# Routing on VectorE alone in four batches, the expert lists made later, and the buffers of the last loads changed, in a two-layer mixture-of-experts trunk

## The chip, the cores and the metric

The kernel runs on one core of one Trainium2 chip. The metric is the device time of one execution in microseconds (us). A core has TensorE (matmuls and transposes; the profile calls it PE, and PEld its weight loads), VectorE (DVE), ScalarE (ACT), GpSimd (POOL) and SyncE (SP). SP issues the plain DMA transfers here, GpSimd the indirect ones (gathers and scatters by a list of indices). Each engine runs its own queue in order.

## The reference

A decoder trunk of two layers over 1024 tokens of width 1024, in float32. Layer 0 mixes the tokens with a gated DeltaNet beside an S5 state space model, layer 1 with dilated attention. After each mixer comes `x = LayerNorm(alpha * x + mixer(x))`, and then the part in question, a mixture of experts in two levels:

```
group_prob = softmax(xt @ wg_r + bg_r);  p_group, group = top_k(group_prob, 1)
in_group   = the 8 logits of (xt @ we_r + be_r) that belong to the group
top_logit, top_local = top_k(in_group, 2)
gate   = p_group * softmax(top_logit);  expert = group * 8 + top_local
y      = sum over the two experts of gate * (silu(x @ w_gate[e]) * (x @ w_up[e])) @ w_down[e]
x      = LayerNorm(alpha * x + y)
```

There are 32 experts with an inner width of 512, so each has 6 MB of float32 weights, and 2048 pairs of token and expert per layer, 64 for an expert in the mean.

## The kernel before, in words

Both layers go through the same stages. **The mixer** fills most of the time that the experts don't take; the change leaves it alone.

**The output stage** (`out_stage`, L816) takes 8 tiles of 128 tokens. For each it adds the residual (L851), takes the row statistics, transposes the tile on TensorE, computes the 36 router logits (`logits`, L250; the sum that ends it is L259), normalizes the tile (`layer_norm`, L217) and stores it to `hd` in main memory. The norm's first step is on ScalarE, its second on VectorE and its third on GpSimd; for the last tile ScalarE takes the second step's scale, and GpSimd both the product with the norm's gain (L223) and the sum (L226). `route` (L261) works on a batch of tiles: for each token the best group and the two best experts by chains of compare and reduce on VectorE (`top`, L279 to 291), the token's rank within its expert by matmuls with a triangle of ones, and the place of its number in a table, with one-hot matrices (L333, L335). `BATCH = {3: 0, 6: 4, 7: 7}` says after which tile a batch is routed and where it begins: tiles 0 to 3, 4 to 6, and 7. The last batch writes the token lists of the first FIXED experts (L353 to 355) and marks the instruction `R["end"]`.

Then come, all in this stage: `sort` (L359), which ranks the 32 experts by count with VectorE ops and matmuls of TensorE and writes the order of the experts and the lists of all others; `gates` (L395), the gate of each pair and its place in a table in memory, with two products on GpSimd (L417); and `overflow` (L682), a chain of small VectorE ops and two matmuls (L712) that lists the blocks of tokens that don't fit.

**The experts** (`moe`, L606). Experts 0 and 1 (FIXED = 2) go first, in fixed order, so that they need no order. The 14 next largest are large like them, up to 128 tokens a pass: each weight tile of 1 MB is split into a high and a low half of fp32r, by a copy on ScalarE (L486) and a difference on VectorE (L489), and each product is three matmuls (L528, L529, L546). The first weight tile's differences go to GpSimd (L488). The 16 others are small: 64 tokens, float32, no split (L583, L599), gathered two at a time in one list. The order is: the fixed ones, then in turn two small and two large. Each expert's rows are gathered from `hd` by an indirect DMA on GpSimd (L495), transposed (L503), and its result is scattered to `yd` by another (L551, L602). After the scatter of the fourth expert, GpSimd issues the 16 scatters of the table (`table`, L422).

All 192 weight tiles of a layer are loaded by SP at L458, in the experts' order, into 17 buffers in turn: RAW = 10 on the left of SBUF, then RAWB = 7 on the right (L455). At most two, later three loads are in flight. For experts past the fixed ones SP first reads the expert's number from the order (L625), and waits for it.

**The join.** A loop over overflow blocks (`moe_rest`, L660) makes no pass with this input, but its start holds all engines at a barrier (L668). Ahead of it stand the loads of the value weights of the attention (`value_loads`, L911, four tiles of 1 MB into buffers of the right ring, layer 0), the loads of rows of `h` (`ahead`, L717) and the splits of the value weights (`value_weights`, L920, through the common `split`, L446: copy L449, difference L450). `combine` (L730) then loads for each token tile its two experts' rows (L738) and normalizes their sum. In layer 0 VectorE adds them (L774, L775), and transposes (L794) and value matmuls follow; in layer 1 TensorE adds them with diagonal matrices (L758), for the odd tiles with alpha times `h` in the same sum (SUMMED). The norm squares the row on ScalarE (L778) and scales it in place on VectorE (L779), then finishes it (L782).

The framework places the instructions: it orders each engine's queue ahead of time by a simulated timeline, sets the semaphores from the tiles' data, and a buffer is free when its last reader is done. `issue_after(x)` keeps instructions behind `x` in that order.

Of the kernel before, what the change touches and what calls it, by code (L numbers as in the profile page):

```python
# [13 lines left out]
I32 = mybir.dt.int32  # L14
# [18 lines left out]
FIXED = 2  # L33
# [5 lines left out]
BATCH = {3: 0, 6: 4, 7: 7}  # L39
# [114 lines left out]
class Trunk:  # L154

    SUMMED = (1, 3, 5, 7)

# [59 lines left out]
    def layer_norm(self, r, mv, g, b, adder, spare=False):  # L217
# [141 lines left out]
    def sort(self, R, first, small, order, ps):  # L359
# [3 lines left out]
        w = R["sort"]  # L363
        key, hot, tmp, tab = w[:NE, 0:32], w[:NE, 32:64], w[:NE, 64:96], w[:NE, 128:256]
        kp, rank = w[:NE, 96:97], w[:NE, 97:98]
        ident = self.ident[:NE, :NE]
        nc.vector.scalar_tensor_tensor(key, R["cnt"][:NE], float(NE), self.c("keyb")[:NE], op0=OP.mult, op1=OP.add)
# [6 lines left out]
        nc.tensor.transpose(p[:NE, :128], R["tab"], self.ident)  # L374
# [8 lines left out]
        nc.vector.tensor_copy(R["rank"], p[:, 96:128])  # L383
# [11 lines left out]
    def gates(self, R, lg, gate, place, wk):  # L395
# [71 lines left out]
    def weights(self, src):  # L467
# [11 lines left out]
        for c in range(2):  # L479
# [126 lines left out]
    def moe(self, l, hd, yd, first, small, order, place, xp, wk, ps):  # L606
# [32 lines left out]
        next(run)  # L639
        next(run)  # L640
        for i in range(NE):
# [12 lines left out]
            if i == 3:  # L654
                with tc.issue_after(st.ins):
                    self.table(l, place)

# [24 lines left out]
    def overflow(self, R, over, ps):  # L682
# [3 lines left out]
        w = R["sort"][:BLOCKS]  # L686
        cap, c, cum, one, le, f = (w[:, i * NE:(i + 1) * NE] for i in range(6))
        ci = R["over"][:BLOCKS]

        idx = self.c("pidx")[:BLOCKS]  # L690
        nc.vector.tensor_scalar(cap, R["rank"][:BLOCKS], float(LARGE) - 0.5, None, op0=OP.is_lt)
# [1403 lines left out]
```

## Time and profile before

| | |
|---|---|
| three runs | 2487.99, 2479.51, 2486.32 us |
| median of the runs | 2486.32 us |
| the profiled execution's own time | 2481.84 us |
| its span in the trace | 2480.0 us |
| mean granted clock of TensorE | 0.961 of full speed |
| busy: TensorE, its weight loads | 2247.2 us (91%), 1629.5 us (66%) |
| busy: VectorE, ScalarE, GpSimd | 1468.4 (59%), 1143.1 (46%), 488.4 us (20%) |
| transfers | 560.83 MB, mean 226 GB/s |

Busy shares are means over the whole span. In it the stretches alternate: in the experts' two stretches, some 545 us each, the transfers run at about 405 GB/s, and in the mixers mostly at 30 to 270. So a share says little of what binds in one stretch, and the rows below are read from stretches: windows of time, the timeline of one engine, and the chain of waits. In a timeline row, the bracket at the end is the engine's idle time ahead of the instruction and what released it; `x8` at the end of the operation says that eight like ones in a row are told as one.

### The profile page before, as it was taken

The page shows a single profiled execution, that of the slowest core. Times are in us where ns is not written, and L with a number is a line of the kernel's source. Part 1 is how long each engine was busy: PE and PEld are TensorE (multiplying, and loading weights), DVE is VectorE, ACT ScalarE, POOL GpSimd, SP SyncE. Part 2 cuts the span into 40 slices and gives each one's busy share as a digit, 9 for nine tenths or more (in the row PEclk, how much of TensorE's full clock was granted, in tenths as well). Part 3 has the DMA queues.
Part 4 walks back from the last instruction along what each step waited for, and adds up shares of the span by engine and source line. Part 5 has one row for each costly group of instructions (what it writes and reads, how often), then busy time and mean ns, then how long its engine had stood idle before and what let it go on. Part 6 is the DMA issues. An engine that isn't in the chain of part 4 may idle for free. (4 is left out here: it accounts for less than half of the span.)

```text
span 2480.0 us, 34001 instructions
## 1 busy us (share of the span) xinstructions
PE 2247.2 (91%) x11950; PEld 1629.5 (66%) x11950; DVE 1468.4 (59%) x2901; ACT 1143.1 (46%) x1871; POOL 488.4 (20%) x566
## 2 busy tenths in 40 slices
PE   7999999889697999999599999998987799999995
PEld 5888899678454555555377888886865555555552
DVE  7655656556853555555553777777567544555545
ACT  5435453442543444444323666667224444444442
POOL 1445434102222111110001111113121311111000
PEclk9999999999698999999799999999988999999998
DMA  4222222272499999999631000102817999999976
GB/s 164 61 65 43 64 82 59 101 267 111 178 390 383 411 406 405 398 405 405 215 123 44 33 30 32 41 25 85 319 59 289 370 415 405 408 408 405 404 286 254
DMA packets 179199, 560.83 MB, mean 226 GB/s; under 512 B 59200, under 2 KB 96448, under 8 KB 129360
## 3 DMA queue, kind: packets, MB, share of 16 engines
q1 hardware_dynamic: 163920, 525.01, 55.6%
q0 software_dynamic: 15104, 33.60, 3.5%
q8 instruction: 96, 1.57, 0.3%
q14 instruction: 79, 0.65, 0.1%
HBM read 518.76 MB, written 55.36 MB: 231 GB/s over the span
## 5 line engine op out<-in xcount | busy, mean ns | idle before, releaser
L489 DVE TENSOR_TENSOR wlo<-wraw,whi 128x1024 fp32r<-128x1024 f32 x380 | 447.9, 1220 | 142.5 <-ACT whi L486 139.2
L486 ACT ACTIVATE whi<-wraw 128x1024 fp32r<-128x1024 f32 x384 | 384.3, 1054 | 74.6 <-PE pu L529 34.6
L583 PE MATMUL pgs<-wraw,xs 128*64 128x512 f32 x1024 | 241.8, 604 | 0.0
L583 PEld LDWEIGHTS pgs<-wraw,xs 128*64 128x64 f32 x1024 | 69.6, 138 | 133.1 <-issue 126.7
L172 PE MATMUL pj<-xTh,phi 128*128 128x512 f32 x320 | 131.0, 414 | 13.3 <-ACT xTh L449 13.3
L1073 POOL TENSOR_TENSOR plo<-praw,phi 128x256 fp32r<-128x256 f32 x64 | 53.0, 829 | 411.0 <-ACT phi L1072 282.1
L172 PE MATMUL pj<-xTh,plo 128*128 128x512 f32 x320 | 132.2, 414 | 0.0
L172 PE MATMUL pj<-xTl,phi 128*128 128x512 f32 x320 | 130.5, 408 | 0.0
L528 PE MATMUL pg<-whi,xh 128*128 128x512 f32 x256 | 107.4, 419 | 20.3 <-ACT whi L486 15.2
L599 PE MATMUL pos<-wraw,hs 128*64 128x512 f32 x512 | 118.6, 598 | 5.1 <-ACT xh L449 3.3
L172 PE MATMUL opo<-ohi,oyp 128*128 128x512 f32 x392 | 115.5, 403 | 2.4 <-DVE oyp L450 2.4
L1089 PE MATMUL pj<-xTh,phi 128*128 128x512 f32 x256 | 114.8, 448 | 2.2 <-DVE KL L1105 1.0
L528 PE MATMUL pg<-wlo,xh 128*128 128x512 f32 x256 | 108.4, 423 | 8.5 <-DVE wlo L489 8.3
L975 ACT ACTIVATE sm<-sm,st 128x1024 f32<-128x1024 f32 (+7 forms) x128 | 99.2, 775 | 36.4 <-DVE st L974 34.9
L551 POOL DMA_INDIRECT yd<-ot,first x32 | 38.8, 1214 | 368.3 <-issue 155.9
L971 DVE CUSTOM_DVE_ANT_0 sm<-s,amask 128x1024 f32<-128x1024 f32 (+7 forms) x128 | 96.4, 755 | 20.9 <-PE s L967 19.0
L988 PE MATMUL pp<-cf,sm 128*128 128x128 f32 x576 | 94.0, 274 | 11.7 <-ACT yt L1013 4.3
L528 PE MATMUL pg<-whi,xl 128*128 128x512 f32 x256 | 103.9, 406 | 0.0
L529 PE MATMUL pu<-wlo,xh 128*128 128x512 f32 x256 | 102.9, 402 | 0.0
L529 PE MATMUL pu<-whi,xl 128*128 128x512 f32 x256 | 102.7, 401 | 0.0
L529 PE MATMUL pu<-whi,xh 128*128 128x512 f32 x256 | 102.4, 400 | 0.0
L1089 PE MATMUL pj<-xTh,plo 128*128 128x512 f32 x256 | 101.5, 397 | 0.1
(543 smaller groups left out, 5148.1 us busy)
## 6 DMA issues: line engine op xcount, KB each, us to landing
wraw<-in_wm SPq DMA_DIRECT2D x384, 1024.0 KB
cy<-yd SPq DMA_DIRECT2D x32, 512.0 KB
praw<-in_win SPq DMA_DIRECT2D x40, 256.0 KB
oraw<-in_wo SPq DMA_DIRECT2D x16, 512.0 KB
hd<-or SPq DMA_DIRECT2D x16, 512.0 KB
ca<-hd SPq DMA_DIRECT2D x16, 512.0 KB
praw<-in_wqk SPq DMA_DIRECT2D x64, 128.0 KB
oy<-ytd SPq DMA_DIRECT2D x14, 448.0 KB
```

What stands on the lines that cost most here:

```text
L172: self.last = self.nc.tensor.matmul(*args, **kw).ins
L486: nc.scalar.activation(hi, r[:, h], AF.Copy)
L489: eng.tensor_tensor(lo, r[:, h], hi.bitcast(F32), op=OP.subtract)
L528: nc.tensor.matmul(pg, x[:, k], w[:, 0:512], start=s, stop=z)
L529: nc.tensor.matmul(pu, x[:, k], w[:, 512:1024], start=s, stop=z)
L583: nc.tensor.matmul(pg[r].rearrange("p (g f) -> p g f", g=2), x[:, k], w[:, k % 2, a], start=(k == 0), stop=(k == KT - 1))
L599: nc.tensor.matmul(po[r], hs[:, f % 2, f // 2], W[f // 2][:, o:o + 512], start=(f == 0), stop=(f == 3))
L971: nc.vector.tensor_tensor_reduce(out=sm[:, :n], in0=s[:, :n], in1=am[:, 1024 - n:1024], scale=1.0, scalar=-3e38, op0=OP.add, op1=OP.max, a ...
L975: nc.scalar.activation(sm[:, :n], sm[:, :n], AF.Exp, bias=st[:, 1:2], accum_out=st[:, 2:3])
L988: nc.tensor.transpose(pp[:, (j - j0) * 128:(j - j0 + 1) * 128], sm[:, j * 128:(j + 1) * 128], self.ident)
L1073: nc.gpsimd.tensor_tensor(lo, r, hi.bitcast(F32), op=OP.subtract)
L1089: nc.tensor.matmul(p, w[:, o], x[:, k, cs], start=(k == 0 and i == 0), stop=(k == KT - 1 and i == 2))
```

## The change

What it does, part by part:

- **Routing.** Four batches in place of three (tiles 0 to 3, 4 and 5, 6, and 7). In `out_stage` a tile's norm and its store now stand ahead of its batch's routing. The last tile's norm is made like the others', with its sum on VectorE. The gates' product and the first weight tile's differences go from GpSimd to VectorE.
- **Late lists.** `sort` is issued in `moe` behind the first expert's gather and its split, and `overflow` behind the table, after the fourth expert; what they read is kept in a tile `ov` that outlives the output stage. FIXED goes from 2 to 3, so the fourth expert, behind which the table is issued, is the first small one.
- **Ring.** The last five weight tiles (from 187 on) use the right ring's buffers. The value weights are loaded straight into `V`, on the left, and split ahead of the loop. The rows of `h` stand first in their pool on the left.
- **Join.** The norm writes its scaled row into `y[:, 1]`, which held the second expert's row, and no longer in place. In layer 1 the loads of the norm's gain and bias, the diagonal matrices, and alpha times `h` for tiles 0 to 3 on TensorE stand ahead of the tiles, and SUMMED is gone.

The diff, cut to its core:

```diff
-FIXED = 2
+FIXED = 3
...
-BATCH = {3: 0, 6: 4, 7: 7}
+BATCH = {3: 0, 5: 4, 6: 6, 7: 7}
...
         last = nc.scalar.activation(r, r, AF.Identity, bias=mv[:, 8:9])
-        if spare:
-            last = nc.scalar.activation(r, r, AF.Copy, scale=mv[:, 7:8])
-            nc.gpsimd.tensor_tensor(r, r, g, op=OP.mult)
-        else:
-            nc.vector.scalar_tensor_tensor(r, r, mv[:, 7:8], g, op0=OP.mult, op1=OP.mult)
+        nc.vector.scalar_tensor_tensor(r, r, mv[:, 7:8], g, op0=OP.mult, op1=OP.mult)
         return last, adder.tensor_tensor(r, r, b, op=OP.add)
...
-            nc.gpsimd.tensor_tensor(M, M, self.c("eidx")[:, None, :].to_broadcast([128, NT, NE]), op=OP.mult)
+            nc.vector.tensor_tensor(M, M, self.c("eidx")[:, None, :].to_broadcast([128, NT, NE]), op=OP.mult)
...
-        raw = self.raw_ring[self.at % len(self.raw_ring)]
+        n = len(self.raw_ring)
+
+        raw = self.raw_ring[self.at % n if self.at < NE * 6 // n * n else -1]
...
-            eng = nc.gpsimd if self.at == 1 else nc.vector
-            with after(eng):
-                eng.tensor_tensor(lo, r[:, h], hi.bitcast(F32), op=OP.subtract)
+            with after(nc.vector):
+                nc.vector.tensor_tensor(lo, r[:, h], hi.bitcast(F32), op=OP.subtract)
...
+        with tc.issue_after(self.hold["x"].ins):
+            self.sort(ov, first, small, order, wk, ps)
         next(run)
...
             if i == 3:
                 with tc.issue_after(st.ins):
                     self.table(l, place)
+                    self.overflow(ov, over, wk, ps)
...
+        P = {}
+        if l:
+            self.bcast_rows(g, self.I["lnfg"][l], D)
+            self.bcast_rows(b, self.I["lnfb"][l], D)
+            al = wk.tile([128, 128], F32, name="al", bufs=1)
+            nc.vector.tensor_scalar(al, self.ident, ALPHA, None, op0=OP.mult)
+            dg = wk.tile([128, NT, 2, 128], F32, name="cdg", bufs=1)
...
+            for u in range(4):
+                P[u] = ps.tile([128, D], F32, name="cp", tag="cp", bufs=4)
+                for c in range(2):
+                    h = slice(c * 512, (c + 1) * 512)
+                    nc.tensor.matmul(P[u][:, h], al, rows[u][:, h], start=True, stop=False)
...
-                if t in self.SUMMED:
-                    terms = [(al, a)] + terms
...
-                if t in self.SUMMED:
+                if t in P:
                     nc.scalar.activation(a, p, AF.Copy, accum_out=st[:, 0:1])
...
-            nc.vector.scalar_tensor_tensor(a, a, st[:, 1:2], g, op0=OP.add, op1=OP.mult)
+            nc.vector.scalar_tensor_tensor(y[:, 1], a, st[:, 1:2], g, op0=OP.add, op1=OP.mult)
...
-            nc.vector.scalar_tensor_tensor(a, a, st[:, 8:9], b, op0=OP.mult, op1=OP.add)
+            nc.vector.scalar_tensor_tensor(a, y[:, 1], st[:, 8:9], b, op0=OP.mult, op1=OP.add)
...
+            act, _ = self.layer_norm(r, mv, g, b, nc.vector if t == NT - 1 else nc.gpsimd)
+            nc.sync.dma_start(hd[ts, :], r)
             if t in BATCH:
                 self.route(BATCH[t], t + 1, R, lg, first, wk, ps)
-            act, add = self.layer_norm(r, mv, g, b, nc.gpsimd, t == NT - 1)
-            nc.sync.dma_start(hd[ts, :], r)
-        R["sort"] = wk.tile([128, KT * 128], F32, name="osort", tag="orT", bufs=1)
         with self.tc.issue_after(R["end"].ins):
-            self.sort(R, first, small, order, ps)
             self.gates(R, lg, gate, place, rp)
-            self.overflow(R, over, ps)
-        self.hold = {nc.scalar: act, nc.gpsimd: add, nc.vector: R["end"]}
+        self.hold = {nc.scalar: act, nc.vector: R["end"]}
...
-    def value_loads(self):
-        R = []
+    def value_weights(self, V, vp):
+
+        W = []
         for a in range(4):
-            r = self.raw_ring[0].tile([128, 2048], F32, name="wraw", tag="wraw")
+            r = V[:, 2 * a:2 * a + 2]
             with self.tc.issue_after(self.flight[-1]):
-                self.nc.sync.dma_start(r, self.I["wv"][a])
...
+                self.nc.sync.dma_start(r.rearrange("p c n -> p (c n)"), self.I["wv"][a])
...
-                        R = self.value_loads()
+                        W = self.value_weights(V, vp)
                     else:
                         vp = alloc("cr")
-
-                        vp.tile([128, 8192 + (NE * 6 % (RAW + RAWB)) * 2048], F32, name="used")
-                    there = self.ahead(l, hd, vp, range(NT if l else 2))
+                    rows = [vp.tile([128, D], F32, name=f"ca{t}") for t in range(NT if l else 2)]
+                    g, b = (vp.tile([128, D], F32, name=n) for n in ("fg", "fb"))
+                    self.ahead(l, hd, rows)
                     self.moe_rest(l, hd, yd, over, xg, wk, ps)
-                    if l == 0:
-                        W = self.value_weights(R, vp)
```

## Rows read from the trace of the kernel before

**Rows 1.** Window in the experts: us, PE, PEld, DVE, ACT, POOL, PEclk, DMA share, GB/s

```profile
700.00:720.00 20.00, 18.36 (x85) 10.72 (x82) 8.40 (x12) 7.51 (x10) 2.27 (x2) 1.00 1.00 403
```

**Rows 2.** Waits in the experts, layer 0: us, times, longest

```profile
SPq L458 <- DMA wraw<-in_wm: 382.1, 169, 4.1
...
PEld pgs L583 <- DMA wraw<-in_wm: 4.7, 15, 0.4
```

**Rows 3.** VectorE's timeline, end of layer 0's routing: start us, us, instruction

```profile
618.54 0.26 DVE L259 SCALAR_TENSOR_TENSOR lg<-lgd,ln_mv,orb 128x36 f32<-128x36 f32 x1
...
625.90 1.63 DVE L259 SCALAR_TENSOR_TENSOR lg<-lgd,ln_mv,orb 128x36 f32<-128x36 f32 x1
...
627.73 2.29 DVE L300 SCALAR_TENSOR_TENSOR rt<-rM,rt 128x96 f32<-128x96 f32 x1
...
629.94 4.71 DVE L317 TENSOR_TENSOR rt<-rM,cf 128x96 bf16<-128x96 f32 x2
...
642.84 0.17 DVE L355 TENSOR_SCALAR first<-first 128x2 int32<-128x2 int32 x1
...
643.19 1.21 DVE L489 TENSOR_TENSOR wlo<-wraw,whi 128x1024 fp32r<-128x1024 f32 x1
...
649.75 0.16 DVE L691 TENSOR_SCALAR osort<-rrank 24x32 f32<-24x32 f32 x1
...
653.08 0.14 DVE L709 TENSOR_SCALAR osort<-osort 24x1 f32<-24x1 f32 x1
```

**Rows 4.** GpSimd's timeline, the same stretch, and layer 1's first gather

```profile
625.11 2.36 POOL L223 TENSOR_TENSOR or<-or,og 128x1024 f32<-128x1024 f32 x1 [5.58 <-ACT or L222]
627.55 2.35 POOL L226 TENSOR_TENSOR or<-or,ob 128x1024 f32<-128x1024 f32 x1
629.87 4.68 POOL L489 TENSOR_TENSOR wlo<-wraw,whi 128x1024 fp32r<-128x1024 f32 x2
...
643.29 3.44 POOL L495 DMA_INDIRECT xg<-hd,first  x1 [1.06 <-DVE ge L408]
...
1866.51 3.34 POOL L495 DMA_INDIRECT xg<-hd,first  x1 [1.04 <-DVE ge L408]
```

**Rows 5.** TensorE's timeline, the first expert's transposes

```profile
653.44 1.97 PE L503 MATMUL px<-cf,xg 128*128 128x128 f32 x8
```

**Rows 6.** SP's timeline, and transfers in 640 to 660 by half microseconds

```profile
650.26 37.61 SPq L458 DMA_DIRECT2D wraw<-in_wm  x14
...
GB/s 0 0 0 0 0 0 0 0 0 0 0 0 0 0 58 74 139 156 49 0 0 0 164 33 229 410 459 410 426 442 393 426 459 410 410 393 377 442 270 271
```

**Rows 7.** GpSimd's and TensorE's timelines around the table, layer 0

```profile
721.58 1.26 POOL L602 DMA_INDIRECT yd<-ots,small  x1 [3.73 <-ACT ots L601]
...
733.80 1.59 POOL L428 DMA_INDIRECT tab<-tokv,place  x1 [0.30 <-issue]
...
756.28 1.05 POOL L495 DMA_INDIRECT xg<-hd,small  x1 [0.30 <-DMA tab<-tokv,place]
...
765.59 1.94 PE L503 MATMUL px<-cf,xg 128*128 128x128 f32 x8 [13.98 <-DMA xg<-hd,small]
```

**Rows 8.** Timelines of ScalarE, SP, VectorE and TensorE at layer 0's join

```profile
1197.44 7.67 ACT L449 ACTIVATE vhi<-wraw 128x1024 fp32r<-128x1024 f32 x8
...
1208.05 0.80 SPq L738 DMA_DIRECT2D cy<-yd  x2
...
1216.24 1.28 DVE L779 SCALAR_TENSOR_TENSOR ca<-ca,fst,fg 128x1024 f32<-128x1024 f32 x1 [1.31 <-ACT cy L778]
...
1222.97 1.97 PE L794 MATMUL ct<-cf,ca 128*128 128x128 f32 x8 [26.12 <-DMA cy<-yd]
```

**Rows 9.** The chain that ended last, and a window of layer 1's join

```profile
2419.40 8.50 DMA fb<-in_lnfb
...
2432.42 36.67 PE cp L758 x80
...
2450.00:2460.00 10.00, 10.00 (x25) 4.46 (x24) 9.37 (x22) 5.13 (x10) 0.00 (x0) 1.00 0.55 222
```

More of the change, by code (lines that the diff above doesn't have):

```diff
@@ L154 @@
 class Trunk:
-    SUMMED = (1, 3, 5, 7)
     def __init__(self, tc, I, out):
@@ L604, in small, with moe @@
             in_=ot, in_offset=None, bounds_check=4 * S - 1, oob_is_err=False)
-    def moe(self, l, hd, yd, first, small, order, place, xp, wk, ps):
+    def moe(self, l, hd, yd, first, small, order, place, ov, over, xp, wk, ps):
         nc, tc = self.nc, self.tc
@@ L680, in moe_rest, with overflow @@
                 pass
[L682 removed]
+    def overflow(self, ov, over, wk, ps):
         nc = self.nc
[L686 to L688 removed]
+        w = wk.tile([NE, 256], F32, name="ovw", tag="ovw", bufs=1)[:BLOCKS]
+        cap, c, cum, one, le, f, ci = (w[:, i * NE:(i + 1) * NE] for i in range(7))
+        ci = ci.bitcast(I32)
+        cnt, rank = ov[:BLOCKS, 0], ov[:BLOCKS, 1]
         idx = self.c("pidx")[:BLOCKS]
[L691 to L692 removed]
+        nc.vector.tensor_scalar(cap, rank, float(LARGE) - 0.5, None, op0=OP.is_lt)
+        nc.vector.scalar_tensor_tensor(c, cap, -64.0, cnt, op0=OP.mult, op1=OP.add)
         nc.vector.tensor_scalar(c, c, 63.0, 0.0, op0=OP.add, op1=OP.max)
@@ L715, in overflow, with ahead @@
         nc.vector.tensor_copy(over[:, 2, 0:1], cum[0:1, NE - 1:NE])
-    def ahead(self, l, hd, p, ts):
+    def ahead(self, l, hd, rows):
         nc = self.nc
-        g, b = (p.tile([128, D], F32, name=n) for n in ("fg", "fb"))
-        rows = {}
         with self.tc.issue_after(self.flight[-1]):
-            for t in ts:
-                rows[t] = p.tile([128, D], F32, name=f"ca{t}")
-                nc.sync.dma_start(rows[t], hd[t * 128:(t + 1) * 128, :])
+            for t, r in enumerate(rows):
+                nc.sync.dma_start(r, hd[t * 128:(t + 1) * 128, :])
                 if l == 0:
-                    nc.scalar.activation(rows[t], rows[t], AF.Copy, scale=ALPHA)
-        return g, b, rows
+                    nc.scalar.activation(r, r, AF.Copy, scale=ALPHA)
     def combine(self, l, hd, yd, gate, g, b, rows, wk, ps, done):
@@ L763, in combine @@
             else:
-                if t in rows:
+                if t < len(rows):
                     a = rows[t]
@@ L814, in out_products, with out_stage @@
                     yield MM, 0
-    def out_stage(self, l, ytd, W, last, po, first_ps, xd, hd, gate, first, small, order, place, over, rp, wk, wp,
+    def out_stage(self, l, ytd, W, last, po, first_ps, xd, hd, gate, first, place, ov, rp, wk, wp,
                   part):
@@ L1983, in run @@
                 with self.pool(f"ow{l}", 2) as wk, self.pool(f"owp{l}") as wp:
-                    self.out_stage(l, ytd, *out, xd, hd, gate, first, small, order, place, over, pools[2], wk, wp,
+                    self.out_stage(l, ytd, *out, xd, hd, gate, first, place, ov, pools[2], wk, wp,
                                    pools[0])
@@ L1993, in run @@
                     self.part_ring = [pools[0]] * 4 + [partb] * 2
-                    xg = self.moe(l, hd, yd, first, small, order, place, xp, wk, ps)
+                    xg = self.moe(l, hd, yd, first, small, order, place, ov, over, xp, wk, ps)
                     for q in reversed(pools):
@@ L2025, in run @@
                     nc.scalar.activation(wk.tile([128, 1], F32, name="warm", bufs=1), self.ident[:, 0:1], AF.Sqrt)
-                    self.combine(l, hd, yd, gate, *there, wk, ps, done)
+                    self.combine(l, hd, yd, gate, g, b, rows, wk, ps, done)
                 vp.release()
```

47 lines of the change are left out of this document (16 added, 31 removed).

## The prediction

> **What bounds the kernel now.** I read the page first and found four stretches in each layer: the mixer, an output stage that ends in routing, the experts, and the join of their rows. The edits sit where one stretch ends and the next starts, so the question for each is which wait ends last there.
>
> In the experts' stage TensorE is busy 18.36 of 20 us and the DMA engines all the time, at 403 GB/s [rows 1]. SP's loads wait for earlier loads, 382.1 us in the first layer, so they are paced by the transfers and not by free buffers; yet the weight loads of TensorE waited only 4.7 us for those transfers in 545 us [rows 2]. Both run at nearly one speed with a cushion of loaded tiles between them. So what starts TensorE earlier, or takes a hole out of its work, moves the end of the stage, as long as the transfers move too.
>
> Ahead of that stage the routing is held up on VectorE. The sum of the logits that took 0.26 us a tile earlier takes 1.63 us, the next op 2.29 and the next two 4.71 [rows 3]. They end at 627.53, 630.02 and 634.65, and GpSimd's ops end at 627.47, 629.90 and 634.55 [rows 4]: each VectorE op waited out a GpSimd op on the same memory. The first expert's list is ready at 643.01 [rows 3], the gather starts at 643.29 [rows 4], its data move from 647 to 649.5 (the slices of half a microsecond in the GB/s row) [rows 6]. But the first transposes start at 653.44 with no wait for a transfer shown [rows 5]: ahead of them in TensorE's queue stood the matmuls of the sort and of the overflow list, whose chain of 17 VectorE ops ran from 649.75 to 653.22 [rows 3]. SP loaded nothing more until 650.26 [rows 6], because it stood at the load of the sorted order. Layer 1 repeats all this 1223.2 us later; its first gather takes 3.34 us [rows 4].
>
> Later, 16 scatters of the table (733.80 to 756) stand on GpSimd's queue ahead of a gather, and TensorE waits 13.98 us for it [rows 7].
>
> At the join of layer 0 the splits of the value weights run on ScalarE from 1197.44 for 7.67 us; only then come the loads of the experts' rows (1208.05), and TensorE stands still for 26.12 us [rows 8]. At the end of layer 1 the loads of the rows wait for the bias row (8.50 us), then TensorE works 36.67 us [rows 9].
>
> **The change, part by part.** All sums are against the profiled execution, 2481.84 us: a span of 2480.0 and 1.84 around it. The median of the three runs, 2486.32, lies 4.48 above it.
>
> *Routing and first gather.* The last tile's norm goes to VectorE: a scale (1.28 us) and a sum (about 1.2, as a weight difference of that size took 1.21 [rows 3]), ready when ScalarE has made one pass over the tile, some 1.2 us ahead of GpSimd's start at 625.11 [rows 4]. So the logits come at 626.8 in place of 625.9 plus 1.63. GpSimd's 2.36 + 2.35 + 4.68 us [rows 4] leave the stretch. What is left of the routing took 8.4 us from 634.6 to 643.0; with tiles 4 and 5 in a batch of their own, and no lock, it is some 15 dependent ops at 0.20 us (17 ops in 3.47 us [rows 3]) and 2 us for ranks and table: 5.2 at least, 8.4 at most, I take 6.4. The list is ready at 633.2, 9.8 earlier. The gather lands 6.2 us after its start at best (643.29 to 649.5) and 10.15 at most (653.44) [rows 4 to 6]; nearest to the data's end I take 7.2, and TensorE starts at 640.7, 12.7 earlier. With the ends: 7.8 to 14.9. I book **12.5 per layer, 25**. The extra batch is some 26 short ops beside TensorE's matmuls, where VectorE is half idle: nothing; without that cover 5 us per layer.
>
> *Late lists.* The sort moves behind the first gather's split, the overflow list behind the fourth expert, and SP's load of the order behind the loads of experts 0 to 2 (the third fixed expert needs no list). SP's queue then holds seven free buffers' worth of loads from about 627. On VectorE the two lists stand between weight differences, on TensorE between matmuls; a weight part is made up to six halves ahead, 8 us of matmuls, which hides their 7 us of VectorE time. At nothing hidden, 23 dependent ops each behind one difference of 1.2 us cost 28 us per layer; at full cover 0. I take the cover: **-1.5 per layer, -3**.
>
> *The table.* It is issued after the fourth expert. With three fixed ones that is the first small expert of a pair, not the second: its scatter came at 721.58 where the table started at 733.80 [rows 7], 12 us earlier as seen from the next gather. The scatter of the second small one now falls behind the table (1.3 us), so the gather comes 9 us earlier as against TensorE, and of the 13.98 us some 5 stay. Below: none is won, if the order on the queue swaps; above: 14. I take **9 per layer, 18**.
>
> *Loads at the end, layer 0.* The last five weight tiles use the seven right buffers, so they wait for the experts before them (until about 1181 on today's clock), and the value weights come behind them, later than now; but their splits no longer wait for the left buffers to be free of TensorE's last matmuls. The last of four tiles lands near 1197, its split ends near 1201, and the barrier at 1202 in place of 1207.8: 5.7. The scale beside the squares, into another tile, takes the 1.31 us wait out of the first tile's chain [rows 8]. Holding the row buffer longer delays the third tile's load by 5 us, behind 11 us of matmuls per tile: nothing; without that cover 5 us once. **7**, from 0 to 8.
>
> *Loads at the end, layer 1.* The eight rows and the two norm rows no longer wait for the buffers of the last weights and start, by the loads ahead of them on SP, some 6 us earlier; so the expert rows start at about 2422 in place of 2427.9, when the bias row is there (2419.40 + 8.50 [rows 9]). Sixteen of TensorE's 80 matmul records go ahead of them into that wait, but then VectorE binds: it is busy 9.37 of 10 us [rows 9] and keeps its work, four tiles at 3.4 us and four at 4.6, 32 us. **6**, from 3 to 10.
>
> Sum: 25 - 3 + 18 + 7 + 6 = 53, and 2481.84 - 53 = **2428.8 us**.
>
> **A rule that speaks against it.** The first gather kept GpSimd for 3.44 us [rows 4] while VectorE worked on weight differences. The Trainium skill (SBUF — State Buffer, section Who interferes with whom) says that VectorE's copies, casts and scalar ops can hold the port through which GpSimd writes descriptors, and that such a transfer then looks blocked; by it the gate ops now beside the gather would delay it. It is the third rival below.
>
> **The rivals.**
> 1. *The transfers pace the experts and do not start earlier*: SP still meets the load of the order first. Then both stages keep their ends and 40 of the 53 go: 2468.8. For it: the full DMA engines [rows 1]; against it: 4.7 us of waiting [rows 2], and that the order is asked for by a later expert. The Trainium skill (SBUF — State Buffer, Summary: rules for kernel authors) would have 358 GB/s from the main memory; 201 MB per layer would by that estimate take 562 us, more than the stage has, and the transfers would be the bound. The row's 403 GB/s decides: 500 us.
> 2. *The hole at the table stays*: 13.98 us again, at another gather: 2446.8. For it: 16 scatters in one row on the queue; against it, the earlier place.
> 3. *The gather starves*: about 20 gate ops of 0.17 us delay it by 3.4 per layer: 2435.6.
> 4. *The end does not come earlier*, since the value weights and rows stand behind five tiles that now wait for buffers: 7 and 6 fall away: 2441.8.
> 5. *The late lists block TensorE* (the slower side). Their matmuls stand in a queue that runs in order; if each of the 23 ops of a layer waits out one difference (1.23 us and its own 0.2), TensorE loses 33 us per layer, 66 in all, for the 3 booked: 2491.8. It decides from 1.4 us per op on. Against it: today two differences stand among the sort's ops and cost 2.4 us in all.
>
> **How the numbers follow.** Forecast 0.50, rival 1 0.12, rival 2 0.14, rival 3 0.09, rival 4 0.10, rival 5 0.05. The bounds of the terms reach from 2481.84 - 25 (7.8 per layer, nothing from the table, 3 at the end, 6 for a half-covered join) to 2481.84 - 75; I take 2408 to 2462, which leaves out most of rival 1, all of rival 5 and the joint extremes, under 2 in 10. A measurement of this kernel can tell about 0.3% (7.4 us) from no change. Slower by that is rival 5 and nothing else: 0.05. Within it are mixtures of rivals 1, 2 and 4 at their worst: 0.03. Faster: 0.92.
>
> **What would show it.** Right: VectorE ops of 0.2 to 0.3 us between the last logits and the list, list to logits 6 to 7 us, the first transposes at about 640.7 in place of 653.44; SP loads before 640; a wait of TensorE for the gather behind the table of about 5 us; the join's idle time of TensorE near 19; the last row loads 6 us sooner after the last scatter. Wrong: long VectorE ops without GpSimd beside them; TensorE waits for VectorE in the first and fourth expert; waits of TensorE for weights late in the stage (rival 1); a wait of 14 us at another gather (rival 2); the forecast falls as a whole if the stage of the experts is as long as now and starts no earlier.

## The result and the profile after

| | before | after |
|---|---|---|
| median of the runs | 2486.70 us (2479.51 to 2487.99, 4 runs) | 2461.63 us (2460.36 to 2462.60, 4 runs) |
| ratio to before, 95% interval | | 0.9905 [0.9885, 0.9924] |
| profiled execution, its span | 2481.84, 2480.0 us | 2461.31, 2459.5 us |

The kernel is faster by 25 us, inside the range by 0.4 us at its slow end, where 53 were forecast. The forecast was counted from the profiled execution; there the time fell from 2481.84 to 2461.31 us, and the spans differ by 20.5 us. Cut at the first transposes of an expert and at the start of the last expert's eviction on ScalarE, they show where that came from:

| stretch | before | after | difference | forecast |
|---|---|---|---|---|
| start to the first expert's transposes, layer 0 | 653.44 | 643.28 | -10.2 | -12.5 |
| experts, layer 0 | 543.50 | 542.44 | -1.1 | -7.5 |
| end of these to the transposes of layer 1 | 679.73 | 669.21 | -10.5 | -19.5 |
| experts, layer 1 | 541.47 | 548.06 | +6.6 | -7.5 |
| end of these to the end | 61.86 | 56.51 | -5.4 | -6 |

So the routing and the end gave most of what was forecast for them, and the experts' stages nothing: they grew by 5.5 us in sum.

*Routing.* VectorE's timeline at the end of layer 0's routing, which answers to [rows 3]:

```profile
626.36 0.25 DVE L252 SCALAR_TENSOR_TENSOR lg<-lgd,ln_mv,orb 128x36 f32<-128x36 f32 x1
626.62 1.22 DVE L219 TENSOR_TENSOR or<-or,ob 128x1024 f32<-128x1024 f32 x1
...
633.54 0.17 DVE L348 TENSOR_SCALAR first<-first 128x3 int32<-128x3 int32 x1
...
633.79 0.76 DVE L410 TENSOR_TENSOR rM<-rM,cf 128x256 f32<-128x256 f32 x2
634.46 4.63 DVE L483 TENSOR_TENSOR wlo<-wraw,whi 128x1024 fp32r<-128x1024 f32 x4
```

The sum of the logits is back at 0.25 us, no op waits for GpSimd any more, and the list is ready at 633.71, 9.3 us earlier. GpSimd's timeline, which answers to [rows 4]:

```profile
636.17 4.01 POOL L489 DMA_INDIRECT xg<-hd,first  x1 [15.58 <-DVE wlo L483]
```

and TensorE's timeline, which answers to [rows 5] and to the last of [rows 7]:

```profile
643.28 1.97 PE L497 MATMUL px<-cf,xg 128*128 128x128 f32 x8 [9.97 <-DMA xg<-hd,first]
...
765.77 1.94 PE L497 MATMUL px<-cf,xg 128*128 128x128 f32 x8 [4.03 <-DMA xg<-hd,small]
```

The gather starts 2.46 us after its list (0.28 before) and its rows let TensorE begin 9.57 us after the list.

*Loads.* SP's timeline, which answers to [rows 6]:

```profile
618.78 9.34 SPq L453 DMA_DIRECT2D wraw<-in_wm  x4
628.22 0.38 SPq L867 DMA_DIRECT2D hd<-or  x1
630.54 48.17 SPq L453 DMA_DIRECT2D wraw<-in_wm  x10
```

SP's waits in layer 0's stage (us, times, longest), which answer to [rows 2]:

```profile
SPq L453 <- DMA wraw<-in_wm: 374.3, 165, 4.1
SPq L619 <- DVE small L384: 24.6, 1, 24.6
SPq L453 <- DVE wlo L483: 17.3, 9, 13.3
```

Six loads more start before SP comes to the order, 31 us earlier than before (618.8 against 650.3). Then SP stands at the order for 24.6 us (19.3 before): load 16 starts at 659.6, and load 28 lands only 5 us before it is used (701.6 and 706.2).

*The table.* GpSimd's timeline, which answers to [rows 7]:

```profile
733.31 1.38 POOL L596 DMA_INDIRECT yd<-ots,small  x1 [5.42 <-ACT ots L595]
735.00 1.09 POOL L421 DMA_INDIRECT tab<-tokv,place  x1 [0.30 <-issue]
...
757.00 1.15 POOL L489 DMA_INDIRECT xg<-hd,small  x1 [0.30 <-issue]
```

The wait behind it is 4.03 us where it was 13.98 (4.0 in layer 1).

*The stages.* Windows of the two stages (columns as in [rows 1]):

```profile
643.28:1185.72 542.44, 504.67 (x2223) 303.25 (x2223) 293.45 (x343) 247.32 (x306) 76.66 (x70) 0.97 0.95 378
1854.93:2402.99 548.06, 503.04 (x2223) 298.89 (x2223) 293.19 (x343) 245.68 (x306) 82.59 (x70) 0.98 0.95 375
```

*The join of layer 0*, which answers to [rows 8]. ScalarE's timeline:

```profile
1185.72 0.60 ACT L595 ACTIVATE ots<-pos 128x512 f32<-128x512 f32 x1 [6.47 <-DMA yd<-ots,small]
1186.22 7.67 ACT L442 ACTIVATE vhi<-V 128x1024 fp32r<-128x1024 f32 x8
```

VectorE's:

```profile
1187.30 9.17 DVE L443 TENSOR_TENSOR vlo<-V,vhi 128x1024 fp32r<-128x1024 f32 x8 [6.63 <-DMA V<-in_wv]
...
1205.38 1.28 DVE L777 SCALAR_TENSOR_TENSOR cy<-ca,fst,fg 128x1024 f32<-128x1024 f32 x1 [1.30 <-DMA fg<-in_lnfg]
...
1207.83 1.29 DVE L780 SCALAR_TENSOR_TENSOR ca<-cy,fst,fb 128x1024 f32<-128x1024 f32 x1
1209.03 1.28 DVE L772 SCALAR_TENSOR_TENSOR ca<-cy,gate,ca 128x1024 f32<-128x1024 f32 x1
```

TensorE's:

```profile
1209.17 1.97 PE L792 MATMUL ct<-cf,ca 128*128 128x128 f32 x8 [24.79 <-DVE ca L780]
```

ScalarE's splits still stand directly behind the last eviction, though the first two of the four tiles of value weights had landed before it, at 1180.4 and 1183.0. VectorE's differences end at 1196.47, and TensorE stands still for 24.79 us, 1.33 less than before. The wait of 1.31 us for the squares is gone, and one of 1.30 us for the gain's row, whose load stands behind those of the first rows, as it did before, is in its place.

*The end*, the chain that ended last, which answers to [rows 9]:

```profile
2403.86 4.20 DMA yd<-ots,small
2409.41 9.45 PE cp L744 x16
2418.85 13.75 PE cp L756 x32
```

No bias row stands in it, and 16 of TensorE's 80 matmul records, those with alpha times `h`, run ahead of the others.

### The profile page after: what moved, and what is told of

Read it like the earlier page. It is cut to its first block, busy times and chain, and to the rows that moved or that the text cites. A ratio compares the mean times of both kernels' runs of the same rounds, so it can differ in the third digit from the quotient of the medians.

```text
span 2459.5 us, 33997 instructions
## 1 busy us (share of the span) xinstructions
PE 2244.8 (91%) x11952; PEld 1629.4 (66%) x11952; DVE 1469.8 (60%) x2963; ACT 1139.4 (46%) x1869; POOL 466.4 (19%) x554
## 5 line engine op out<-in xcount | busy, mean ns | idle before, releaser
L169 PE MATMUL pj<-xTh,phi 128*128 128x512 f32 x320 | 130.7, 413 | 13.2 <-ACT xTh L442 13.2
L522 PE MATMUL pg<-wlo,xh 128*128 128x512 f32 x256 | 111.1, 434 | 10.8 <-DVE wlo L483 10.4
L962 ACT ACTIVATE sm<-sm,st 128x1024 f32<-128x1024 f32 (+7 forms) x128 | 99.1, 775 | 36.6 <-DVE st L961 35.3
L523 PE MATMUL pu<-whi,xl 128*128 128x512 f32 x256 | 103.0, 402 | 0.0
```

The source lines that it names most:

```text
L169: self.last = self.nc.tensor.matmul(*args, **kw).ins
L522: nc.tensor.matmul(pg, x[:, k], w[:, 0:512], start=s, stop=z)
L523: nc.tensor.matmul(pu, x[:, k], w[:, 512:1024], start=s, stop=z)
L962: nc.scalar.activation(sm[:, :n], sm[:, :n], AF.Exp, bias=st[:, 1:2], accum_out=st[:, 2:3])
```

## The experiments

Three theories of what paces the experts' stage, since that is where the forecast failed: **A**, the transfers; **B**, TensorE with its own waits, the one at the table among them; **C**, the order that the framework writes for ScalarE's splits. The stage is told in four sections between starts of ScalarE's evictions: A1, from the first transposes to the fifth expert in the order (the second small one); A2, to the eleventh (the gather behind the table lies here in the changed kernel); A3, to the 27th, four groups of two large and two small; A4, to the last. Lengths in us, layer 0 / layer 1:

| kernel | A1 | A2 | A3 | A4 | stage |
|---|---|---|---|---|---|
| changed kernel | 101.1 / 99.4 | 105.1 / 105.3 | 265.9 / 274.1 | 70.3 / 69.2 | 542.4 / 548.1 |
| nudge | 102.9 / 99.4 | 106.1 / 106.5 | 269.0 / 274.5 | 69.8 / 69.3 | 547.9 / 549.6 |
| in_place | 101.5 / 102.7 | 108.2 / 104.7 | 266.0 / 274.3 | 69.6 / 69.3 | 545.3 / 551.1 |
| table_second | 101.0 / 99.1 | 104.9 / 106.9 | 267.3 / 275.6 | 69.2 / 69.3 | 542.4 / 550.9 |
| first_gp | 100.2 / 101.3 | 109.1 / 108.8 | 267.2 / 272.5 | 69.1 / 68.5 | 545.6 / 551.1 |
| table_late | 101.3 / 103.0 | 98.3 / 94.6 | 262.9 / 267.1 | 71.6 / 69.2 | 534.1 / 533.8 |
| table_20 | 102.0 / 100.2 | 99.6 / 94.6 | 263.7 / 269.8 | 69.2 / 69.6 | 534.5 / 534.2 |
| order_early | 100.5 / 99.8 | 98.7 / 95.7 | 278.7 / 267.7 | 70.7 / 70.6 | 548.6 / 533.9 |
| both | 100.0 / 100.4 | 91.4 / 90.7 | 263.0 / 261.0 | 69.2 / 71.1 | 523.7 / 523.2 |
| split_ahead | 95.7 / 98.5 | 112.4 / 100.6 | 272.9 / 268.8 | 66.7 / 70.0 | 547.7 / 537.9 |
| split_ahead_late | 96.8 / 98.7 | 103.2 / 97.2 | 273.1 / 272.9 | 74.9 / 71.1 | 548.0 / 539.8 |
| half_loads | 96.8 / 95.3 | 123.2 / 121.9 | 252.3 / 252.5 | 62.1 / 59.2 | 534.3 / 528.9 |

**order_early**: the sort is issued right behind the last list.

```diff
-        next(run)
-        with tc.issue_after(self.hold["x"].ins):
+        with tc.issue_after(self.hold[nc.vector].ins):
             self.sort(ov, first, small, order, wk, ps)
         next(run)
+        next(run)
```

> The changed kernel with the sort issued as soon as the counts are there, ahead of the first expert's gather and split, while the overflow list stays late. In the changed kernel SP waited 24.6 us for the order in layer 0 and 21.5 us in layer 1, with the DMA engines idle. Theory A (the transfers pace the experts; what the change gained in TensorE's start and at the table was lost because the transfers start only some 12 us earlier): the sort fits into the 9.6 us in which the gather is awaited, the loads from the 16th on come 10 to 17 us earlier per layer, and the stage ends 6 to 12 us earlier: 2437 to 2450 us in place of 2461.6. Theory B (TensorE with its own waits and its granted clock paces them, and the loads have a cushion of 16 to 25 us anyway): the loads come earlier, but the stage of layer 0 stays 542 us long and the time within 4 us of 2461.6.

Measured: 2448.97 us (2442.39 to 2453.14), 0.9844 [0.9813, 0.9874]. SP's waits in layer 0's stage:

```profile
SPq L453 <- DMA wraw<-in_wm: 364.7, 158, 5.7
SPq L453 <- DVE wlo L483: 39.1, 15, 22.7
...
SPq L619 <- DVE small L384: 10.4, 1, 10.4
```

The wait for the order falls from 24.6 to 10.4, and the section A2 from 105 to 98.7 and 95.7 us, though in layer 0 TensorE still waits 5.0 us behind the table. In layer 0 all of that was lost again in A3, with loads that had landed 19 to 32 us ahead of their use: A alone does not explain it.

**table_late**: the table goes behind the 29th expert, the overflow list stays.

```diff
             if i == 3:
                 with tc.issue_after(st.ins):
-                    self.table(l, place)
                     self.overflow(ov, over, wk, ps)
+            if i == 28:
+                with tc.issue_after(st.ins):
+                    self.table(l, place)
```

> The changed kernel with the 16 scatters of the table issued behind the 29th expert, when no gather is left on GpSimd's queue (before: behind the 4th); the overflow list stays. The wait of TensorE for the gather behind the table, 4.0 us in the changed kernel, goes. Theory A (transfers pace): the time stays, 2457 to 2464. Theory B (TensorE paces): the 4 us per layer and the lower granted clock that follows the wait come back, 2447 to 2455.

Measured: 2431.48 us (2429.47 to 2434.73), 0.9775 [0.9750, 0.9800], 30 us below the changed kernel and less than either theory expected. No gather waits for the table. The stages lose 8.3 and 14.2 us, 6.8 and 10.7 of them in A2.

**table_second**: the same edit with `i == 4` for the table.

> The changed kernel with the table issued behind the fifth expert, the second small one of the pair, where the kernel before had it. The hole of about 14 us in TensorE's work should be back in the trace. Theory A (transfers pace): the hole is made up by the end of the stage, and the time stays within 4 us of 2461.6. Theory B (TensorE paces): the 10 us by which the hole was shortened in each layer are lost again, 2476 to 2484. The prediction's term for the table (9 us per layer) stands or falls with this.

Measured: 2457.41 us (2456.30 to 2464.34), 0.9891 [0.9863, 0.9919], as the changed kernel. The wait is not gone, it moved to the next gather, that of a large expert; TensorE's timeline:

```profile
781.65 1.94 PE L497 MATMUL px<-cf,xg 128*128 128x128 f32 x8 [4.15 <-DMA xg<-hd,first]
```

The hole of 14 us that was expected did not come, so this run does not show what such a hole is worth. It does show what the wait of 4.15 us is worth by itself: in layer 0, from the first transposes to the end of A2, ScalarE and VectorE work in the same order here, in table_late and in table_20 (below), and TensorE too but for the place of one gather's transposes. A2 is 104.9 us with the wait and 98.3 and 99.6 without it, so there it costs 5.2 to 6.6 us (one profile of each).

**half_loads**: each weight load moves only the first half of its tile, and both halves are computed from it. So the weights' second halves are left out, layer 1 routes other data, and its overflow loop may run; only the stages are read.

```diff
-            ld = nc.sync.dma_start(r, src)
+            ld = nc.sync.dma_start(r[:, 0:1024], src[:, 0:1024])
...
```

> The changed kernel, where each load of a weight tile of the experts moves only the first half of its columns (512 KB in place of 1 MB), and both halves of the work are done on that half; so the computation of the experts is another one, of the same size on every compute engine. Read in layer 0, since the routing of layer 1 changes with the data. Theory A (transfers pace): the stage of layer 0, from the first transposes to the last expert, 542 us now, shrinks by 20 us or more. Theory B (TensorE paces): it stays within 5 us of 542.

Measured: 2458.36 us, one run. Windows of the two stages:

```profile
643.45:1177.80 534.35, 497.19 (x2223) 304.10 (x2223) 303.02 (x351) 264.15 (x317) 80.05 (x70) 0.98 0.66 214
1840.04:2368.93 528.89, 496.62 (x2223) 303.61 (x2223) 293.71 (x344) 254.30 (x307) 80.25 (x70) 0.98 0.67 220
```

TensorE's timeline behind the table:

```profile
758.32 1.94 PE L497 MATMUL px<-cf,xg 128*128 128x128 f32 x8 [14.01 <-DMA xg<-hd,first]
```

With the transfers at 0.66 of the time and 214 GB/s the stage is only 8 and 19 us shorter, in spite of a wait of 14 us behind the table. TensorE's 497 us of work are the least that any run showed (both, below, has as many), and A3 at 252 us shows groups without a wait for a split. Since the framework writes another order for shorter loads, this run can't tell the transfers' part from the order's.

**split_ahead**: a large expert's third weight tile is split ahead of the pause between its halves, for theory C in one form (six splits that stand late). **split_ahead_late** adds the edit of table_late.

```diff
             if k == KT // 2:
+                W2 = self.weights(wsrc(k // 2))
                 yield
-            if k % 2 == 0:
+                W = W2
+            elif k % 2 == 0:
                 W = self.weights(wsrc(k // 2))
```

> The changed kernel, where a large expert's third weight tile is loaded and split one step earlier in the program, ahead of the second half of the expert before it; the table stays behind the fourth expert, and all amounts of work stay. In half_loads a group of four experts (two small, two large) took 63.1 us in the middle of the stage, where the changed kernel takes 64.6 to 69.2; in table_late with full transfers two groups of layer 0 took 63.1 too, and these two have six splits ahead of the second small expert's eviction on ScalarE's queue, the others four. Theory C (the order in which the splits stand on ScalarE's queue, planned ahead of time, paces the experts): groups of 63 to 66 us, and 2425 to 2450 us in place of 2461.6. Theory A (transfers pace): groups of 66 to 68 us as before, 2457 to 2466.

> split_ahead and table_late together: early splits, and the table behind the 29th expert. Theory C: the wait behind the table goes as in table_late (30 us there), and the groups take 63 to 66 us: 2405 to 2430. Theory A: no less than table_late, 2429 to 2436.

Measured: 2457.40 us (2452.64 to 2459.14), 0.9874 [0.9848, 0.9900], and 2450.21 us (2449.19 to 2457.59), 0.9846 [0.9823, 0.9869]. TensorE's waits from 840 to 1160 in split_ahead:

```profile
PE pg L524 <- ACT whi L481: 8.5, 5, 1.7
PE po L542 <- ACT whi L481: 6.5, 4, 1.6
```

A miss: the waits for splits are no shorter than in the changed kernel (8.4 and 1.6 there), nor is A3 in layer 0, and with the late table the kernel is 19 us slower than without the edit. That form of C falls.

**before_table_late**: the kernel before with its table behind the 29th expert (the same edit).

> The kernel before the change, with the table alone moved behind the 29th expert; this measures what the 13.98 us hole of the prediction was worth in the kernel before. If the term of the prediction is right in kind (the hole lies on TensorE's path and comes back whole), 2455 to 2462 in place of 2487. If the groups after the hole took back what it cost (the group behind it took 60.3 us, later ones 65 to 69.5), or if the planned order of the queues moves more than the hole does, 2475 to 2495.

Measured: 2479.46 us (2468.54 to 2485.71, 10 runs), 0.9965 [0.9947, 0.9982]. The waits of 14.0 and 13.2 us are gone, but the stages are shorter by 1.9 and 6.5 us only: the six experts around the table take 12.7 us less (layer 0, 110.5 to 97.8), the four groups behind them 10.6 more (264.9 to 275.5). In the kernel before, the groups behind the hole gave back what it cost, or the order did: ScalarE's queue has another order in them in the two kernels, and no run tells these apart. The changed kernel with the same edit is 48 us faster than this one.

**in_place**: the norm scales in place again.

```diff
-            nc.vector.scalar_tensor_tensor(y[:, 1], a, st[:, 1:2], g, op0=OP.add, op1=OP.mult)
+            nc.vector.scalar_tensor_tensor(a, a, st[:, 1:2], g, op0=OP.add, op1=OP.mult)
...
-            nc.vector.scalar_tensor_tensor(a, y[:, 1], st[:, 8:9], b, op0=OP.mult, op1=OP.add)
+            nc.vector.scalar_tensor_tensor(a, a, st[:, 8:9], b, op0=OP.mult, op1=OP.add)
```

> The changed kernel, with the norm's scale written in place again, as before the change. Nothing else in the join changes, and nothing in the experts of layer 0. If the second row's buffer, held longer by the scale beside the squares, is what gives back 3 us in the value stage (its first matmul came 13.8 us earlier than before the change, its last ones 11.0), the value stage ends 2 to 3 us earlier and the first transposes of the join 1.3 us later. If it is not, the value stage ends as now or later. The experts of layer 1 have the same work; by theory C their time may still move by some us when the planned order of ScalarE's queue comes out differently there, by theory A it stays within 2 us of 548.

Measured: 2462.56 us (2457.97 to 2465.52), 0.9898 [0.9871, 0.9925]: in the whole time that part of the change is worth nothing that can be told. In the join of layer 0 it is worth something: from the end of the experts to the first transposes it is 26.28 us here, 23.45 in the changed kernel and 26.03 before the change. But from there to layer 1's logits it is 7 us less here (623.0 against 630.1; the other kernels with full loads that keep this part of the change lie between 624.6 and 630.8). At the start of the stage the first transposes came 3.2 us earlier, and the wait behind the table took most of it back:

```profile
764.97 1.94 PE L497 MATMUL px<-cf,xg 128*128 128x128 f32 x8 [6.39 <-DMA xg<-hd,small]
```

**both**: order_early and table_late together.

> The sort right behind the last list (as in order_early) and the table behind the 29th expert (as in table_late). Theory B (TensorE with its own waits paces the experts; the earlier loads are only more cushion): no more than table_late gave, 2426 to 2437, stage lengths 531 to 539 in both layers. If the loads' 16 us for the order did cost something that the hole at the table covered up in order_early, the two gains add: 2431.5 less some 12, about 2419.

Measured: **2413.41 us** (2412.41 to 2419.51), 0.9711 [0.9695, 0.9727], the fastest kernel of the study, 48 us below the changed kernel; the two gains alone, 12.7 and 30.2, add to 42.9. The "no more than table_late" of theory B is wrong. Its stages, with the transfers busy for 0.99 of the time:

```profile
644.10:1167.77 523.67, 496.98 (x2214) 298.81 (x2212) 291.99 (x336) 247.92 (x306) 82.49 (x70) 0.99 0.99 390
1831.46:2354.66 523.20, 496.45 (x2214) 296.46 (x2212) 291.93 (x336) 247.02 (x306) 84.55 (x70) 0.99 0.99 393
```

What it saves in A2 is seen side by side. The changed kernel's windows behind the table:

```profile
744.00:764.00 20.00, 17.44 (x76) 13.77 (x76) 15.68 (x15) 12.65 (x14) 12.17 (x11) 1.00 0.97 332
764.00:784.00 20.00, 18.23 (x80) 9.69 (x81) 3.43 (x6) 2.77 (x5) 2.81 (x3) 0.91 1.02 419
784.00:804.00 20.00, 17.19 (x71) 8.53 (x70) 7.88 (x10) 7.04 (x10) 3.29 (x4) 0.83 1.01 406
804.00:824.00 20.00, 17.79 (x71) 11.99 (x70) 12.15 (x12) 12.14 (x14) 0.99 (x1) 0.91 1.01 401
```

and those of both:

```profile
744.00:764.00 20.00, 18.75 (x88) 14.93 (x90) 17.04 (x18) 14.47 (x18) 5.04 (x4) 1.00 1.01 412
764.00:784.00 20.00, 20.00 (x90) 9.37 (x88) 4.74 (x7) 5.70 (x8) 0.00 (x0) 1.00 1.01 409
784.00:804.00 20.00, 20.00 (x92) 11.60 (x89) 13.44 (x15) 9.86 (x12) 4.29 (x3) 1.00 1.01 420
804.00:824.00 20.00, 19.75 (x98) 15.57 (x98) 13.40 (x15) 11.78 (x15) 4.98 (x4) 1.00 1.01 411
```

Over A2 of layer 0, TensorE is idle for 10.3 us and busy for 94.9 in the changed kernel (744.33 to 849.48), idle for 2.1 and busy for 89.3 in both (744.13 to 835.50): of the 13.8 us, 8.2 are waits, and in 5.6 TensorE is busy for longer, at a granted clock of 0.94 against 1.00 over the section.

**nudge**: one memset of 8 columns on VectorE per layer, work that nobody waits for.

```diff
             scat.append(st)
+            if i == 4:
+                nc.vector.memset(wk.tile([128, 8], F32, name="nud", bufs=1), 0.0)
```

> The changed kernel plus one memset of 8 columns on VectorE behind the fifth expert's scatter, work of some 0.15 us per layer that nobody waits for. By the framework's order ScalarE's queue in layer 1 is the same as in the changed kernel, in layer 0 it is another from the ninth expert on. Theory C (the planned order of the queues sets the pace): layer 1's stage 548 within 1.5, layer 0's moves away from 542.5 by 2 us or more. Theory B without the order: both stages within 1.5 us of 542.5 and 548.1, the time 2461.6 within 3.

Measured: 2466.84 us (2466.56 to 2467.27), 0.9919 [0.9903, 0.9936]. The expectation's premise was wrong: the memset was placed early, and the orders of ScalarE, VectorE and GpSimd are otherwise the changed kernel's in both layers. So it tells nothing on C by a change of order. It is nearly a repeat, and it lies 5.2 us higher (stages +5.4 and +1.5), with no overlap of the runs. The changed kernel was not run again beside it, so the memset and the occasion are not told apart (the kernel before had 2486.70 us beside the one and 2486.95 beside the other). Differences of some 5 us between two kernels' whole times are not read as an effect.

**table_20**: the table behind the 21st expert.

> The table behind the 21st expert in place of the 29th. A wait of some 4 us of TensorE for the gather behind it comes back, at a later place. If a wait adds its length to the stage: 4 us per layer over table_late, about 2440. If the groups behind a wait pay it back, as they did in before_table_late: 2431.5 within 3. If only the place early in the stage does harm: as table_late. If the gain of table_late is a matter of the order that the framework happened to find: anything from 2431 to 2460, with no wait behind the table that explains it.

Measured: 2435.00 us (2423.24 to 2438.55), 0.9780 [0.9751, 0.9809], as table_late. No wait came back: the 16 scatters (1005.35 to 1031.3) found a stretch in which no gather was due. So the table costs nothing that can be told where no gather waits for it, and two positions without a wait give stages of 534 us, within 0.7, in both layers.

**first_gp**: the first weight tile's two differences go to GpSimd, behind the gather.

```diff
-            with after(nc.vector):
-                nc.vector.tensor_tensor(lo, r[:, h], hi.bitcast(F32), op=OP.subtract)
+            eng = nc.gpsimd if self.at == 1 else nc.vector
+            with after(eng):
+                eng.tensor_tensor(lo, r[:, h], hi.bitcast(F32), op=OP.subtract)
```

(and `hold` keeps the gather, so that GpSimd's work stands behind it).

> In the changed kernel the first gather starts 2.46 us after its list and takes 4.01 us, while VectorE runs four weight differences. Here the first weight tile's two differences go to GpSimd behind the gather, so that VectorE has short ops and later two differences. If VectorE's differences hold the gather up: it starts within 1 us of its list and takes 3.4 us or less, and the first transposes come 2 to 3 us earlier, 640.5 to 641.5, if GpSimd's two differences (2.35 us each) land before TensorE wants them. If the delay is the gather's own: the same 9.5 us from list to transposes, 643.3. The total is within 6 us of the changed kernel's either way.

Measured: 2460.12 us (2456.07 to 2461.85), 0.9887 [0.9870, 0.9903]. GpSimd's timeline, layer 0 and layer 1:

```profile
636.14 1.46 POOL L490 DMA_INDIRECT xg<-hd,first  x1 [16.34 <-DVE wlo L484]
...
1847.57 2.10 POOL L490 DMA_INDIRECT xg<-hd,first  x1 [13.84 <-DVE rM L410]
```

Inconclusive. From the list to the transposes it is 9.52 us in layer 0 (9.57 in the changed kernel) and 7.33 in layer 1 (9.47). The gather's own time on GpSimd fell from 4.01 to 1.46 us in layer 0, yet its start there is no earlier, 3.2 us behind its list, with a VectorE difference as the releaser. In layer 1 of the changed kernel the gather starts 0.81 us behind its list and takes 2.11 us, and the 9.47 us pass all the same: neither its start nor its time on GpSimd is the whole cause.

## Why the prediction was right and wrong

**The direction and the range** held, the range by 0.4 us, which was luck: the size was wrong by more than half, at two steps.

**The table, "9 per layer, 18", failed**, though its mechanism came as told: 4.03 us of wait where "some 5 us stay" was forecast. What failed is the sentence under all the sums, that what "takes a hole out of its work, moves the end of the stage". In the kernel before, taking the whole hole out (before_table_late) shortened the stages by 1.9 and 6.5 us, not by 14 and 13. In the changed kernel the remaining 4 us cost more than their length: 5.2 to 6.6 us of A2 in layer 0, where the order of the queues is the same with and without them. The stages without them (table_late, table_20) were 8 to 14 us shorter, but A3 has other orders there, so how much of that is the wait's is not shown. Only rival 1 put the hole's worth at nothing, and that by the transfers; the others asked how long the wait would be, and none what a wait is worth.

**Late lists, "-1.5 per layer", failed.** TensorE did not wait for the lists, as forecast (rival 5 did not come). But "SP's load of the order behind the loads of experts 0 to 2" was wrong: expert 3's first tiles are loaded ahead of expert 2's last two, so SP had six loads more to make and then stood at the order for 24.6 and 21.5 us. Rival 1 had the wait right and its price wrong: order_early gives 12.7 us, and with the table out of the way (both against table_late) 18. So the step was worth about -6 to -9 per layer, an estimate from these two differences that holds the changed order of the queues with it.

**Routing and first gather, 12.5 per layer**: the list came 9.3 us earlier (9.8 forecast); in layer 1 the time from the last sum of the logits to the list, start to start, fell by 10.9 (16.93 to 6.07). The gather took 9.57 us to TensorE's start in place of 7.5: two thirds of what rival 3 would cost, but that VectorE's ops are the cause is not shown (first_gp). So 10.2 came. (The lower bound of 5.2 us for the routing adds up to 5.0 from its own terms; nothing hangs on it.)

**The join of layer 0, "7, from 0 to 8"**: from the end of the experts to the first transposes 26.03 became 23.45, that is 2.6. Its first term, 5.7, came to nothing: the loads of the experts' rows start 11.10 us after the last eviction, 11.11 before. Failed: "their splits no longer wait for the left buffers". They start 0.50 us after the last eviction, as before, because they stand behind it in ScalarE's queue. The 2.6 came with the second term, the scale into another tile, but by luck: the 1.31 us were replaced by the 1.30 us wait for the gain's row, and instead VectorE now ends the first tile's norm (L780 at 1207.83) before it adds the second tile's rows (L772). Before, two such adds stood ahead of the end of the norm, the second of them here:

```profile
1220.04 1.28 DVE L775 SCALAR_TENSOR_TENSOR ca<-cy,gate,ca 128x1024 f32<-128x1024 f32 x1
...
1221.63 1.28 DVE L782 SCALAR_TENSOR_TENSOR ca<-ca,fst,fb 128x1024 f32<-128x1024 f32 x1
```

With the scale in place again (in_place) the adds are back ahead of it, and the 26.28 us with them. The rest of that stretch, to layer 1's logits, took 3.9 us more than before, and 3.5 to 5.4 more than in table_late and both, with the same code; the cause stays open.

**The end, 6**: 5.4, right. The loads of the experts' rows start 5.78 us after the last eviction, 10.31 before.

**Pace.** "Both run at nearly one speed with a cushion" stands. Of the theories, A alone falls with half_loads and order_early, and B has to be widened: with the wait behind the table gone and SP's wait for the order down to 10.2 and 9.0 us, the stages are 19 and 25 us shorter (both), 13.8 and 14.6 us of it in A2. C is left open, but the runs point to it. Where ScalarE's and VectorE's queues have the same order in A3, its length is nearly the same, whatever the kernel and the layer. One order took 265.9 to 269.0 us in layer 0 of five kernels (the changed one, nudge, in_place, table_second, first_gp) and 267.1 in layer 1 of table_late. A second took 272.5 to 275.6 in layer 1 of four of the five (all but in_place). A third took 272.9 in layer 0 of split_ahead and in layer 1 of split_ahead_late. With other orders A3 lies between 261 and 279, with the same work. But no run changed the order and nothing else, so the order as the cause is not shown.

## What to carry to other kernels

A wait's length in a profile is not its price: try the kernel with the wait moved out of the stage, on both sides of a change, before it is booked, and compare stretches in which the engines' queues have the same order. Work that nobody needs soon (a table of indices) belongs where no gather stands behind it, and what SP must wait for (the order) belongs as early as its data allow, even at the cost of a few short ops. When an edit takes one wait out of a chain, look for the next one that stands there already, as the gain's row did.

## What was not expected of the hardware

In these windows the granted clock fell behind short waits. Windows of the changed kernel around the wait of 4.03 us, and behind waits of 0.94 and 1.05 us at 795 and 796:

```profile
764.00:766.00 2.00, 0.23 (x1) 0.27 (x2) 0.00 (x0) 0.00 (x0) 0.00 (x0) 0.86 1.03 426
766.00:768.00 2.00, 2.00 (x10) 1.60 (x11) 0.26 (x1) 1.03 (x2) 0.00 (x0) 0.50 1.02 424
768.00:770.00 2.00, 2.00 (x9) 0.52 (x6) 1.03 (x2) 0.16 (x1) 1.23 (x2) 0.78 1.01 422
...
796.00:798.00 2.00, 1.65 (x8) 1.57 (x8) 0.00 (x0) 0.53 (x2) 0.00 (x0) 0.54 1.00 410
798.00:800.00 2.00, 1.22 (x4) 0.50 (x2) 1.65 (x2) 2.00 (x4) 1.04 (x1) 0.50 1.04 406
800.00:802.00 2.00, 1.96 (x5) 1.39 (x5) 2.00 (x4) 2.00 (x3) 0.00 (x0) 0.50 1.00 406
802.00:804.00 2.00, 2.00 (x8) 1.54 (x8) 2.00 (x3) 0.34 (x1) 0.00 (x0) 0.75 1.00 404
```

0.50 is the lower level, 1.2 GHz, for some 3 and 7 us with TensorE busy in most of them. The Trainium skill (TensorE: Matmul & The Clock Gate, section HAM oscillation — how this bites in real kernels) describes waits for transfers after which the next work starts on the lower clock; the trace agrees for the wait of 4.03 us for the gather (0.50 from 766 to 768). Around the fall at 796 it is another case: from 770 to 800 TensorE's longest wait is 1.05 us, and the one just ahead of it, 0.94 us, is for VectorE.

The second surprise is the spread between kernels: with one memset of 8 columns per layer more, and the order of ScalarE, VectorE and GpSimd otherwise the same, the median lay 5.2 us higher, with every run of one kernel outside the runs of the other. Whether the memset did it is not shown, since the changed kernel was not run again beside it.
